# A decoder step on one core: a weight ring of four units instead of five, and sample attention over eight sequences in one go

## The chip, the core and the metric

The kernel runs on one core of a Trainium2 chip. The metric is device time of one execution in microseconds (us). A few per cent of the matmul records may be missing from a trace.

## The reference: what is computed

Two decoder layers work on 1024 new prompt tokens and on 8 sampled sequences of 8 tokens, all in float32 with a model width of 1024. In each layer x is normalized, mixed over tokens (layer 0: a gated linear recurrence, "rg"; layer 1: chunked gated linear attention, "gla"), then goes through cross-attention to 256 memory tokens in 4 heads of width 256, then through an MLP with a hidden width of 4096.

```python
def cross_attn(xn, k, v, w_q, w_o):
    q = (xn @ w_q).reshape(B, T, XA_HEADS, XA_HD)
    s = jnp.einsum('bthd,bmhd->bhtm', q, k) * (XA_HD ** -0.5)
    p = jax.nn.softmax(s, axis=-1)
    o = jnp.einsum('bhtm,bmhd->bthd', p, v).reshape(B, T, D_MODEL)
    return o @ w_o
...
x = x + mixer(rmsnorm(x, norm_mix_g[layer]))
x = x + cross_attn(rmsnorm(x, norm_xa_g[layer]), mem_k[layer], mem_v[layer], xa_wq[layer], xa_wo[layer])
hid = rmsnorm(x, norm_mlp_g[layer]) @ mlp_w1[layer]
x = x + jnp.square(jax.nn.relu(hid)) @ mlp_w2[layer]
```

The prompt attends to memory keys and values that this step computes from mem_prompt. Each of the 8 sampled sequences attends to its own cached keys and values (cache_mem_k, cache_mem_v), 256 KB a sequence and head for the keys and as much for the values.

## The kernel before, in words

All 1088 token columns stay resident as x transposed, in three chunks (c = 0, 1, 2) of 384, 384 and 320 columns; the last has 256 columns of the prompt and the 64 sampled ones. Each float32 GEMM is three matmuls, since operands are split into a high and a low part: high by high (L99), low by high (L100) and, with the low part of the weights, high by low (L101). Tiles xh and xl (or hh and hl) are the halves of the activations, whi and wlo those of the weights.

Weights come as units of 128 by 1024 floats (512 KB). `pump` loads a unit from HBM into a staging buffer `raw` (SP issues the DMA) and, as soon as the unit RING before it has been freed, splits it: ACT casts it to whi (L186), DVE subtracts to get wlo (L187). RING is the number of split units that fit (L145). There is one staging buffer of the ring's own, and each phase may add some of its own pool (`new_phase(name, more_raw)`). `get` hands out the next two units, `free` gives two back.

`gemm_in` (48 matmuls a chunk into the PSUM banks pa) makes a projection of a chunk. `gemm_out` (48 matmuls into pb) is the way back; DVE adds each of its groups into x (L279). Out projections aren't run where their operands are made: `queue_out` puts them on a list, and `pop` runs the oldest where the program wants work for PE. The phases run in the order memory keys and values, rg, attention 0, MLP 0, gla, attention 1, MLP 1. Instructions are issued in program order as far as the scheduling of the tile framework keeps it, and each engine runs its own in order.

The recurrence `rg` goes over four groups g of 256 channels. Per group and chunk there are X (a projection and a convolution), G (gates: 12 matmuls against gate weights gwh and gwl into the banks pm, then sigmoid, exp, tanh and square root on ACT, and a scan on DVE) and Y (a second projection, gelu, a product into hh and hl), and then an out projection is queued. ACT loads a table whenever the function's family changes. PE's clock can be granted at 2.4 GHz or at half of it; the profile gives it as a share of full speed.

The attention `xattn` goes over 4 heads h and 3 chunks c. Per item there are Q (projection), `scores` and softmax, `p_trans` (L774), `p_v`, and the queued out projection. The sampled columns are treated with the last chunk: `sample_s` multiplies each sequence's queries qs (padded to 32 columns) with its keys, `sample_p` is the softmax, `sample_v` transposes P (`turn`, L809), multiplies it as pt with the values and turns the result again. The product is `dot4` (L801): for four sequences side by side in the array's column quarters, two matmuls of 128 by 32 weights and 256 columns each; a matmul shows as two records. A key or value tile is `kvt`, loaded by `load` (L706); there are six such buffers, and the memory's own keys and values (out_mem_kT, out_mem_v) pass through them too.

```python
L798        def dot4(out, o, lhs, rhs):
L799            for s in range(2):
L800                for i in range(4):
L801                    nc.tensor.matmul(out[i * 32:i * 32 + 32, o * 256:o * 256 + 256], lhs(s, i), rhs[i][:, s, :],
L802                                     start=s == 0, stop=s == 1)
```

Of the kernel before, what the change touches and what calls it, by code (L numbers as in the profile page):

```python
# [8 lines left out]
F32 = mybir.dt.float32  # L9
# [13 lines left out]
NC = len(COL)  # L23
# [4 lines left out]
MAXW = max(WID)  # L28
# [19 lines left out]
class Step:  # L48
# [95 lines left out]

    RING = 5  # L145

# [378 lines left out]
    def rg(self, next_norm):  # L525
        nc, a = self.nc, self.a
        self.new_phase("rg")
        halo = self.t("halo", [128, 2, 3])
# [3 lines left out]
        def Y(us, us_o, g, c):  # L532
            p = self.gemm_in(us, c)
            if c == NC - 1:
                self.free(us)
            w = WID[c]
            z = self.t("gy", [128, 2, MAXW])[:, :, :w]
            for f in range(2):
                nc.vector.tensor_mul(z[:, f], p[f][:, :w], self.rstd[c])
            gelu = nc.scalar.activation(z, z, AF.Gelu_apprx_tanh)  # L540
            if (g, c) == (3, NC - 1):
                self.table(gelu)
            nc.vector.tensor_mul(z, z, xc.pop(c)[:, :, :w])
            hT = self.hidden()
            nc.scalar.copy(hT[0][:, :, :w], z)
            nc.vector.tensor_sub(hT[1][:, :, :w], z, f32(hT[0][:, :, :w]))
            self.queue_out(us_o, hT, c, next_norm if g == 3 else None)
# [81 lines left out]

        for g in range(4):  # L630
            us_x = self.get()
            us_o = []
# [7 lines left out]
            G(gw, g, 0)  # L640
            self.pop()
            us_y = self.get()
# [47 lines left out]
    def xattn(self, l, next_norm):  # L690
        nc, a = self.nc, self.a
# [5 lines left out]
        st = {}  # L697
# [4 lines left out]

        def load(src):

            t = self.t("kvt", [128, 2, 256], F32, 6)
            nc.sync.dma_start(t, src.rearrange("(t p) c -> p t c", p=128))  # L706
            return t

        def load_split(src, tag):
            raw = load(src)  # L710
            hi = self.t(tag + "h", [128, 2, 256], R32)
            lo = self.t(tag + "l", [128, 2, 256], R32)
            split(hi, lo, raw)
            return hi, lo
# [76 lines left out]

        def keys4(h, o):
            return [load(a.cache_kT[l, o * 4 + i, h]) for i in range(4)]

        def vals4(h, o):
            return [load(a.cache_v[l, o * 4 + i, h]) for i in range(4)]

        def dot4(out, o, lhs, rhs):  # L798
            for s in range(2):  # L799
                for i in range(4):  # L800
                    nc.tensor.matmul(out[i * 32:i * 32 + 32, o * 256:o * 256 + 256], lhs(s, i), rhs[i][:, s, :],  # L801
                                     start=s == 0, stop=s == 1)  # L802

# [8 lines left out]

        def sample_s(h, o, k4):
            if o == 0:
                st["s"] = self.pb()
            dot4(st["s"], o, lambda s, i: qs[:, s, o * 4 + i, :], k4)

# [4 lines left out]

        def sample_v(h, P, hT):
            p = turn(P)
            pt = self.t("pt", [128, 2, 2, 128])
            nc.scalar.copy(pt, p)
            so = self.pb()
            for o in range(2):
                dot4(so, o, lambda s, i: pt[:, s, o, i * 32:i * 32 + 32], vals4(h, o))
            ot = self.t("q", [128, 2, MAXW])[:, :, 0:256]  # L830
# [13 lines left out]
        for n, (h, c) in enumerate(items):  # L844
# [4 lines left out]
            tail = c == NC - 1  # L849
            if tail:  # L850
                k4 = keys4(h, 0)
            if nxt:
# [4 lines left out]
            if tail:  # L857
                sample_s(h, 0, k4)
                k4 = keys4(h, 1)
                sample_s(h, 1, k4)  # L860
                P = sample_p(h)
            else:
                self.pop()
# [5 lines left out]
            if tail:  # L869
                sample_v(h, P, hT)  # L870
                self.pop()
# [362 lines left out]
```

## Time and profile before

| what | before |
|---|---|
| median of 3 runs | 3126.18 us (3124.58 to 3127.01) |
| the profiled execution's own time | 3127.53 us |
| its span in the trace | 3125.8 us |
| mean granted clock of PE | 0.995 of full speed |
| loads and stores in HBM | 178.34 MB read, 13.52 MB written |
| memory keys and values | from 7.6 to 115 us |
| rg | to about 440 us |
| attention 0, MLP 0 | to about 715 us, to about 1480 us |
| gla, attention 1 | to about 2050 us, to about 2345 us |
| MLP 1 | to the end |

The stages' limits are read from PE's blocks in the timeline. PE, PEld, DVE, ACT, POOL and SP are the engines: matmuls, weight loads (they run beside matmuls), vector, scalar, the general engine and the one that issues DMAs. In the rows below, a timeline's row gives the start, the duration, the engine, the line, the operation, out<-in by tile names, sizes and a count of consecutive records; a pipelined matmul's duration is longer than the distance to the next one's start, so distances between starts are what adds up.

### The profile page before, as it was taken

Reading aid. Unit: us, or ns where it says so; the run is one execution under the profiler, and the core shown is the slowest. Engines: PE = TensorE matmul, PEld = TensorE weight load, DVE = VectorE, ACT = ScalarE, POOL = GpSimd, SP = SyncE. Lnnn points to the kernel's source line nnn. Section 1 sums busy time; section 2 is a strip of 40 time slices with the busy share of each in tenths; the row PEclk is TensorE's granted clock in tenths of the full one; section 3 lists DMA queues with packets and bytes.
Section 4 is the critical chain, followed back from the end, with each engine's and each line's share of the span. In section 5 each row is a group of like instructions: output and inputs, shape, how many; then the busy total and the mean of one; then the engine's idle time right before and its main releaser. Section 6 shows DMA issues by size and latency. Waiting matters only on the chain.

```text
span 3125.8 us, 46516 instructions
## 1 busy us (share of the span) xinstructions
PE 3072.0 (98%) x19319; PEld 2932.3 (94%) x19319; DVE 1743.6 (56%) x3266; ACT 1017.9 (33%) x1847; POOL 197.1 (6%) x274
## 2 busy tenths in 40 slices
PE   8999999999999999999999999999999999999997
PEld 7999989989999999999889888798989999999997
DVE  7577785566444444445454454675565444444445
ACT  7555572234211211113333233442243111111114
POOL 3111020001000000001000000010010000000002
PEclk9999999999999999999999999999999999999998
DMA  8311113331111111111011102023331111111111
GB/s 272 116 43 43 41 56 102 95 101 62 49 47 41 47 49 41 41 52 45 28 57 42 56 28 70 24 81 103 108 94 48 48 41 41 54 42 41 43 46 58
DMA packets 155779, 194.85 MB, mean 62 GB/s; under 512 B 11280, under 2 KB 140560, under 8 KB 155568
## 3 DMA queue, kind: packets, MB, share of 16 engines
q1 hardware_dynamic: 152768, 182.82, 18.8%
q0 software_dynamic: 2800, 9.06, 0.8%
q8 instruction: 151, 2.47, 0.3%
q14 instruction: 60, 0.49, 0.1%
HBM read 178.34 MB, written 13.52 MB: 61 GB/s over the span
## 4 chain that ended last, share of the span: by engine, by line
PE 88%; DVE 4%; DMA 3%; ACT 3%; issue 1%; POOL 0%; SPq 0%; DVEq 0%; ACTq 0%; POOLq 0%
PE pa L100 11%; PE pa L99 11%; PE pa L101 11%; PE pb L99 9%; PE pb L101 8%; PE pb L100 8%; PE pm L99 4%; PE pm L100 4%; PE pm L101 4%; PE pa L262 2%; PE pa L264 2%; PE pa L263 2%; PE pb L801 1%; PE pm L1034 1%; DVE wlo L187 1%
## 5 line engine op out<-in xcount | busy, mean ns | idle before, releaser
L100 PE MATMUL pa<-xl,whi 128*128 128x384 f32 (+2 forms) x2336 | 762.4, 326 | 4.4 <-DVE xl L312 4.4
L99 PE MATMUL pa<-xh,whi 128*128 128x384 f32 (+2 forms) x2336 | 762.2, 326 | 2.9 <-DVE xs L565 1.5
L101 PE MATMUL pa<-xh,wlo 128*128 128x384 f32 (+2 forms) x2336 | 761.2, 326 | 0.0
L279 DVE TENSOR_TENSOR x<-x,pb 128x384 f32<-128x384 f32 (+1 forms) x792 | 411.2, 528 | 228.8 <-PE pb L101 228.4
L99 PE MATMUL pb<-hh,whi 128*128 128x384 f32 (+1 forms) x1584 | 523.5, 332 | 2.4 <-DVE x L279 2.4
L100 PE MATMUL pb<-hl,whi 128*128 128x384 f32 (+1 forms) x1584 | 520.7, 329 | 0.0
L101 PE MATMUL pb<-hh,wlo 128*128 128x384 f32 (+1 forms) x1584 | 518.3, 328 | 0.0
L186 ACT CAST whi<-raw 128x1024 fp32r<-128x1024 f32 (+1 forms) x250 | 257.4, 1041 | 666.0 <-PE pa L100 349.6
L187 DVE TENSOR_TENSOR wlo<-raw,whi 128x1024 fp32r<-128x1024 f32 (+1 forms) x250 | 304.4, 1228 | 264.1 <-ACT whi L186 263.2
L100 PEld LDWEIGHTS pa<-xl,whi 128*128 128x128 f32 x2336 | 439.0, 188 | 9.8 <-DVE xl L312 6.3
L99 PEld LDWEIGHTS pa<-xh,whi 128*128 128x128 f32 x2336 | 439.2, 188 | 8.5 <-issue 4.4
L101 PEld LDWEIGHTS pa<-xh,wlo 128*128 128x128 f32 x2336 | 439.2, 188 | 0.8 <-issue 0.8
L679 DVE SCALAR_TENSOR_TENSOR r<-pa,rstd 128x384 f32<-128x384 f32 (+1 forms) x192 | 102.2, 534 | 394.4 <-PE pa L101 394.3
L99 PEld LDWEIGHTS pb<-hh,whi 128*128 128x128 f32 x1584 | 297.6, 188 | 15.8 <-DVE x L279 7.8
L100 PEld LDWEIGHTS pb<-hl,whi 128*128 128x128 f32 x1584 | 298.4, 188 | 5.2 <-issue 4.9
L101 PEld LDWEIGHTS pb<-hh,wlo 128*128 128x128 f32 x1584 | 298.2, 188 | 3.8 <-issue 3.7
L680 ACT ACTIVATE r<-r 128x768 f32<-128x768 f32 (+1 forms) x96 | 77.6, 808 | 670.9 <-DVE r L679 670.9
L279 DVE TENSOR_TENSOR x<-x,pm 128x320 f32<-128x320 f32 (+1 forms) x360 | 190.9, 530 | 112.1 <-PE pm L101 111.8
L306 POOL TENSOR_TENSOR acc<-acc,sq 128x384 f32<-128x384 f32 (+1 forms) x105 | 115.7, 1102 | 2082.0 <-ACT sq L305 2051.6
L99 PE MATMUL pm<-hh,whi 128*128 128x320 f32 (+1 forms) x720 | 234.6, 326 | 0.0
L101 PE MATMUL pm<-hh,wlo 128*128 128x320 f32 (+1 forms) x720 | 234.5, 326 | 0.0
L100 PE MATMUL pm<-hl,whi 128*128 128x320 f32 (+1 forms) x720 | 234.5, 326 | 0.0
(305 smaller groups left out, 4356.9 us busy)
## 6 DMA issues: line engine op xcount, KB each, us to landing
raw<-in_mlp_w SPq DMA_DIRECT2D x128, 512.0 KB, 3.8
kvt<-in_cache_kT SPq DMA_DIRECT2D x64, 256.0 KB, 3.8
kvt<-in_cache_v SPq DMA_DIRECT2D x64, 256.0 KB, 3.7
raw<-in_xa_wv SPq DMA_DIRECT2D x16, 512.0 KB, 5.2
raw<-in_rg_w_in SPq DMA_DIRECT2D x16, 512.0 KB, 3.6
raw<-in_xa_wq SPq DMA_DIRECT2D x16, 512.0 KB, 3.5
raw<-in_xa_wo SPq DMA_DIRECT2D x16, 512.0 KB, 3.5
raw<-in_gla_w_in SPq DMA_DIRECT2D x16, 512.0 KB, 3.7
```

The lines of the kernel that those rows point to most:

```text
L99: mm(out, lh, rh, start=first, stop=False)
L100: mm(out, lh, rl, start=False, stop=False)
L101: mm(out, ll, rh, start=False, stop=last)
L186: nc.scalar.copy(hi[:, o], raw[:, o])
L187: nc.vector.tensor_sub(lo[:, o], raw[:, o], f32(hi[:, o]))
L262: mm(out, self.xh[c][:, k, xs], hv[:, kk, :], start=k == 0, stop=False)
L263: mm(out, self.xh[c][:, k, xs], lv[:, kk, :], start=False, stop=False)
L264: mm(out, self.xl[c][:, k, xs], hv[:, kk, :], start=False, stop=k == 7)
L279: nc.vector.tensor_add(x, x, p[:, :per * w].rearrange("p (m t) -> p m t", m=per))
L306: (nc.vector if m % 4 == 3 else nc.gpsimd).tensor_add(self.acc[c][:, :w], self.acc[c][:, :w], sq[:, :w])
L679: nc.vector.scalar_tensor_tensor(r[:, f], p[f][:, :w], 0.0, self.rstd[c], op0=OP.max, op1=OP.mult)
L680: nc.scalar.activation(r, r, AF.Square)
```

## The change

The ring of split weights has four units instead of five, which frees 8 KB in each of the 128 partitions. The attention has eight key and value buffers `kvt` instead of six; the memory's own keys and values pass through a buffer of their own, `kvr`. The sampled products of all eight sequences stand in one loop (`dots`, matmul at L800 now), for which all eight keys are loaded one chunk earlier and all eight values right behind the scores. In the recurrence the phase has a second staging buffer, `gy` has two buffers, and one of the three places where a queued out projection is run moves to the front of each group. Line numbers from 801 on become smaller by one to four.

```diff
--- before.py
+++ after.py
@@ -142,7 +142,7 @@
                 rows(a.mlp_w2[l], g * 256)
         self.units = u
 
-    RING = 5
+    RING = 4
 
     def pump(self, loads=None, also=None):
         nc = self.nc
@@ -524,7 +524,7 @@
 
     def rg(self, next_norm):
         nc, a = self.nc, self.a
-        self.new_phase("rg")
+        self.new_phase("rg", 1)
         halo = self.t("halo", [128, 2, 3])
         self.stage = self.t("stage", [128, NK, 36])
         xc, xcs = {}, {}
@@ -534,7 +534,7 @@
             if c == NC - 1:
                 self.free(us)
             w = WID[c]
-            z = self.t("gy", [128, 2, MAXW])[:, :, :w]
+            z = self.t("gy", [128, 2, MAXW], F32, 2)[:, :, :w]
             for f in range(2):
                 nc.vector.tensor_mul(z[:, f], p[f][:, :w], self.rstd[c])
             gelu = nc.scalar.activation(z, z, AF.Gelu_apprx_tanh)
@@ -628,6 +628,7 @@
                 nc.gpsimd.tensor_copy(st[:, :, 27:35], h[:, :, 256:320].rearrange("p f (b t) -> p f b t", b=8)[:, :, :, 7])
 
         for g in range(4):
+            self.pop()
             us_x = self.get()
             us_o = []
             X(us_x, g, 0)
@@ -638,7 +639,6 @@
             self.tick()
             self.pop()
             G(gw, g, 0)
-            self.pop()
             us_y = self.get()
             Y(us_y, us_o, g, 0)
             self.tick()
@@ -700,14 +700,14 @@
             nc.scalar.copy(ch, src)
             nc.vector.tensor_sub(cl, src, f32(ch))
 
-        def load(src):
-
-            t = self.t("kvt", [128, 2, 256], F32, 6)
+        def load(src, tag="kvt", bufs=8):
+
+            t = self.t(tag, [128, 2, 256], F32, bufs)
             nc.sync.dma_start(t, src.rearrange("(t p) c -> p t c", p=128))
             return t
 
         def load_split(src, tag):
-            raw = load(src)
+            raw = load(src, "kvr", 1)
             hi = self.t(tag + "h", [128, 2, 256], R32)
             lo = self.t(tag + "l", [128, 2, 256], R32)
             split(hi, lo, raw)
@@ -789,17 +789,16 @@
             return hT
 
 
-        def keys4(h, o):
-            return [load(a.cache_kT[l, o * 4 + i, h]) for i in range(4)]
-
-        def vals4(h, o):
-            return [load(a.cache_v[l, o * 4 + i, h]) for i in range(4)]
-
-        def dot4(out, o, lhs, rhs):
-            for s in range(2):
-                for i in range(4):
-                    nc.tensor.matmul(out[i * 32:i * 32 + 32, o * 256:o * 256 + 256], lhs(s, i), rhs[i][:, s, :],
-                                     start=s == 0, stop=s == 1)
+        def eight(cache, h):
+            return [load(cache[l, b, h]) for b in range(8)]
+
+        def dots(out, lhs, rhs):
+
+            for o in range(2):
+                for s in range(2):
+                    for i in range(4):
+                        nc.tensor.matmul(out[i * 32:i * 32 + 32, o * 256:o * 256 + 256], lhs(o, s, i),
+                                         rhs[o * 4 + i][:, s, :], start=s == 0, stop=s == 1)
 
         def turn(src):
 
@@ -810,23 +809,21 @@
                                         self.ident)
             return p.rearrange("p (s o c) -> p s o c", s=2, o=2)
 
-        def sample_s(h, o, k4):
-            if o == 0:
-                st["s"] = self.pb()
-            dot4(st["s"], o, lambda s, i: qs[:, s, o * 4 + i, :], k4)
+        def sample_s(h, keys):
+            st["s"] = self.pb()
+            dots(st["s"], lambda o, s, i: qs[:, s, o * 4 + i, :], keys)
 
         def sample_p(h):
             P = self.t("P", [128, 3, 256])[:, 0:2, :]
             softmax(st.pop("s"), P)
             return P
 
-        def sample_v(h, P, hT):
+        def sample_v(h, P, vals, hT):
             p = turn(P)
             pt = self.t("pt", [128, 2, 2, 128])
             nc.scalar.copy(pt, p)
             so = self.pb()
-            for o in range(2):
-                dot4(so, o, lambda s, i: pt[:, s, o, i * 32:i * 32 + 32], vals4(h, o))
+            dots(so, lambda o, s, i: pt[:, s, o, i * 32:i * 32 + 32], vals)
             ot = self.t("q", [128, 2, MAXW])[:, :, 0:256]
             nc.vector.tensor_copy(ot, so.rearrange("p (a b) -> p a b", a=2))
             p = turn(ot)
@@ -847,17 +844,16 @@
                 uo = None
             nxt = items[n + 1] if n + 1 < len(items) else None
             tail = c == NC - 1
-            if tail:
-                k4 = keys4(h, 0)
+            if c == NC - 2:
+                keys = eight(a.cache_kT, h)
             if nxt:
                 self.need(nxt[1], norm)
                 Q(*nxt)
                 self.tick()
             p_trans(h, c)
             if tail:
-                sample_s(h, 0, k4)
-                k4 = keys4(h, 1)
-                sample_s(h, 1, k4)
+                sample_s(h, keys)
+                vals = eight(a.cache_v, h)
                 P = sample_p(h)
             else:
                 self.pop()
@@ -867,7 +863,7 @@
                     st["k"] = load_split(a.mem_kT[l, nxt[0]], "k")
                 scores(*nxt)
             if tail:
-                sample_v(h, P, hT)
+                sample_v(h, P, vals, hT)
                 self.pop()
             if uo is None:
                 uo = self.get()
```

How instructions move, at three places. First PE in the attention, the end of the scores of head 1 in layer 0 (kvt are keys, qs padded queries, hh and vh the prompt's P and memory values, xh and whi those of the next query projection). Before:

```order
L99 MATMUL pa<-xh_90,whi 128x384
L801 MATMUL pb<-kvt,qs 32x256
L100 MATMUL pa<-xl_93,whi 128x384
L101 MATMUL pa<-xh_90,wlo 128x384
L99 MATMUL pa<-xh_90,whi 128x384
L100 MATMUL pa<-xl_93,whi 128x384
L101 MATMUL pa<-xh_90,wlo 128x384
L801 MATMUL pb<-kvt,qs 32x256 x5
L99 MATMUL pa<-xh_90,whi 128x384
```

In the changed kernel, from the end of the query projection on:

```order
L101 MATMUL pa<-xh_89,wlo 128x384
L774 MATMUL pm<-ident,P 128x128 x4
L800 MATMUL pb<-kvt,qs 32x256 x16
L99 MATMUL pm<-hh,vh 128x256
L100 MATMUL pm<-hl,vh 128x256
L101 MATMUL pm<-hh,vl 128x256
L99 MATMUL pm<-hh,vh 128x256
```

The sixteen matmuls that stood as ten, one and five between GEMM matmuls stand in one row. Behind it there are 12 `p_v` matmuls, 12 score matmuls, 2 of the query projection, 6 of the scores, the transposes of P, 12 of the query projection, and then the sixteen for the values. Before, 29 matmuls of the query projection stood between the first scores piece and the first values piece, and now 14.

Second, SP's queue in the attention, one head (raw are weight units). Before:

```order
L706 DMA kvt<-in_cache_kT 128x2x256 x2
L706 DMA kvt<-out_mem_kT 128x2x256
L706 DMA kvt<-in_cache_v 128x2x256 x8
L706 DMA kvt<-out_mem_v 128x2x256
L706 DMA kvt<-in_cache_kT 128x2x256 x6
L165 DMA raw<-in_mlp_w 128x4x256 x2
```

In the changed kernel:

```order
L706 DMA kvr<-out_mem_v 128x2x256
L706 DMA kvt<-in_cache_v 128x2x256 x8
L706 DMA kvr<-out_mem_kT 128x2x256
L706 DMA kvt<-in_cache_kT 128x2x256 x8
L173 DMA raw<-in_xa_wo 128x1024
L165 DMA raw<-in_xa_wq 128x4x256 x2
```

The eight keys go out in one row behind the values of the head before, and the eight values in one row behind the memory's values; each value load waits for the matmul of the scores that used its buffer.

Third, ACT in the recurrence, group 0 around the gates of chunk 1 (L600 are the sigmoids, L186 the casts of weight units, L545 the cast of Y's result). Before:

```order
L611 ACT_TABLE_LOAD
L611 ACTIVATE rt<-rt 128x768
L348 COPY rstd_97<-pm 128x320
L186 CAST whi<-raw 128x1024
L600 ACT_TABLE_LOAD
L600 ACTIVATE rt<-pm,vec 128x384
L600 ACTIVATE it<-pm,vec 128x384
L600 ACTIVATE rt<-pm,vec 128x384
L600 ACTIVATE it<-pm,vec 128x384
L545 CAST hh<-gy 128x768
```

In the changed kernel:

```order
L611 ACT_TABLE_LOAD
L611 ACTIVATE rt<-rt 128x768
L348 COPY rstd_97<-pm 128x320
L186 CAST whi<-raw 128x1024 x2
L600 ACT_TABLE_LOAD
L600 ACTIVATE rt<-pm,vec 128x384
L600 ACTIVATE it<-pm,vec 128x384
L545 CAST hh<-gy 128x768
L600 ACTIVATE rt<-pm,vec 128x384
L600 ACTIVATE it<-pm,vec 128x384
```

Two casts of weight units, where one stood, are now ahead of the sigmoid's table load, and Y's cast stands between the sigmoids.

## Rows read from the trace of the kernel before

**Rows 1.** The page: busy time and share of the span by engine.

```profile
PE 3072.0 (98%) x19319; PEld 2932.3 (94%) x19319; DVE 1743.6 (56%) x3266; ACT 1017.9 (33%) x1847; POOL 197.1 (6%) x274
```

**Rows 2.** Waits of PE, whole span: us in total, times, longest us.

```profile
PE pb L801 <- DMA kvt<-in_cache_v: 1.3, 2, 0.9
...
PE pb L801 <- DMA kvt<-in_cache_kT: 0.5, 3, 0.2
```

**Rows 3.** Timeline of PE, layer 0, values of head 1: start us, duration us, instruction.

```profile
581.28 0.33 PE L99 MATMUL pa<-xh,whi 128*128 128x384 f32 x1
581.45 0.34 PE L100 MATMUL pa<-xl,whi 128*128 128x384 f32 x1
581.74 1.49 PE L801 MATMUL pb<-kvt,pt 128*32 128x256 f32 x20
...
583.44 0.34 PE L100 MATMUL pb<-hl,whi 128*128 128x384 f32 x1
...
585.37 0.34 PE L99 MATMUL pb<-hh,whi 128*128 128x384 f32 x1
585.64 0.62 PE L801 MATMUL pb<-kvt,pt 128*32 128x256 f32 x2
...
586.47 0.34 PE L101 MATMUL pb<-hh,wlo 128*128 128x384 f32 x1
...
586.84 0.34 PE L100 MATMUL pb<-hl,whi 128*128 128x384 f32 x1
587.11 1.05 PE L801 MATMUL pb<-kvt,pt 128*32 128x256 f32 x10
...
588.36 0.34 PE L99 MATMUL pb<-hh,whi 128*128 128x384 f32 x1
```

**Rows 4.** Timeline of PE, scores of the same head.

```profile
568.99 1.49 PE L801 MATMUL pb<-kvt,qs 128*32 128x256 f32 x20
...
572.82 0.62 PE L801 MATMUL pb<-kvt,qs 128*32 128x256 f32 x2
...
574.46 1.05 PE L801 MATMUL pb<-kvt,qs 128*32 128x256 f32 x10
```

**Rows 5.** Timeline of SP's queue, value loads of the same head.

```profile
571.57 12.14 SPq L706 DMA_DIRECT2D kvt<-in_cache_v  x8
```

**Rows 6.** Windows: length, busy us (PE, PEld, DVE, ACT, POOL), PEclk, DMA share, GB/s.

```profile
40.00:60.00 20.00, 14.46 (x105) 14.29 (x104) 16.48 (x25) 15.11 (x30) 9.10 (x9) 0.84 0.98 329
499.70:505.30 5.60, 5.42 (x40) 3.48 (x34) 1.72 (x3) 1.07 (x4) 0.00 (x0) 1.00 0.61 187
505.30:511.20 5.90, 5.90 (x42) 5.90 (x42) 3.60 (x10) 3.08 (x12) 0.00 (x0) 1.00 0.69 222
506.00:511.00 5.00, 5.00 (x38) 5.00 (x37) 2.75 (x9) 2.48 (x11) 0.00 (x0) 1.00 0.80 256
```

**Rows 7.** A split and a GEMM's start in the MLP (timeline); a load (page).

```profile
904.13 1.23 DVE L187 TENSOR_TENSOR wlo<-raw,whi 128x1024 fp32r<-128x1024 f32 x1 [0.45 <-ACT whi L186]
...
911.34 0.33 PE L99 MATMUL pa<-xh,whi 128*128 128x384 f32 x1
...
raw<-in_xa_wq SPq DMA_DIRECT2D x16, 512.0 KB, 3.5
```

**Rows 8.** Recurrence: timelines of ACT and PE, one window (columns as in rows 6).

```profile
153.94 1.05 ACT L186 CAST whi<-raw 128x1024 fp32r<-128x1024 f32 x1
155.01 1.28 ACT L600 ACT_TABLE_LOAD   x1
...
272.73 0.44 PE L99 MATMUL pb<-hh,whi 128*128 128x384 f32 x1 [0.41 <-DVE x L279]
...
159.30:162.80 3.50, 3.50 (x13) 3.50 (x13) 3.50 (x11) 3.47 (x5) 1.72 (x3) 0.51 0.42 140
```

**Rows 9.** Start of the kernel: timelines of DVE and PE.

```profile
51.30 1.77 DVE L187 TENSOR_TENSOR wlo<-raw,whi 128x1024 fp32r<-128x1024 f32 x1
...
55.16 0.87 PE L347 MATMUL pm<-ident,rtok 128*128 128x128 f32 x3 [5.54 <-DVE rtok L330]
```

## What the change does to the time: a prediction

> **What bounds the kernel now.** I read the page's busy times first. TensorE (PE) is busy 98% of the span, every other engine 56% or less [rows 1]; the idle rest is 3125.8 − 3072.0 = 54 us. Read alone, that row says that no change can win more than 54 us. But a busy PE need not be a full PE, so the second view is what it waits for where the change works: the attention's sample dots at L801 wait 1.8 us in all for their DMAs [rows 2]. A change that only removed these waits would win 1.8 us.
>
> So third, the timeline of PE where the change works. A GEMM matmul of 384 columns starts 0.17 us after the one before it (581.28 to 581.45) [rows 3]. The sample dots use a quarter of the array each (128x32) and run side by side. Their records come as pieces of 20, 2 and 10 (two records to a matmul) with GEMM matmuls between [rows 3, 4]. A piece costs what the start-to-start distance of the GEMM matmuls around it exceeds the usual 0.173: for 20 records 583.44 − 581.45 − 0.35 = 1.64 us, for 2 records 586.47 − 585.37 − 0.35 = 0.75, for 10 records 588.36 − 586.84 − 0.35 = 1.17: 3.56 us for 16 matmuls [rows 3]. They fit a fixed 0.32 for a piece and 0.22 for each step of up to four matmuls side by side and two records deep (6, 2 and 4 steps: 1.64, 0.76, 1.20). PE shows as busy in all of it: the gain, if there is one, lies inside the busy time.
>
> The Trainium skill says so too, in Perfetto Trace Analysis, section Identifying the Most-Contended Engine: matmul busy share is no good measure of the distance to the limit, and weight-load busy share is one of the better ones. Here that share is 94%, which leaves 194 us [rows 1]; by the rule 54 us is no ceiling, by the busy row it is.
>
> **The change, part by part.** *Sample dots in one go.* Sixteen matmuls back to back are 8 steps instead of 12, and one piece instead of three: 1.64 + 2 × 0.22 = 2.08 us instead of 3.56, so 1.5 us a block. In the scores the pieces of 2 and 10 are cut in the same way [rows 4]. There are 16 blocks (2 layers, 4 heads, scores and values): −24 us. Bounds: had the one piece to be priced by the row of 20 records pro rata, it were 1.64 × 32 / 20 = 2.62 and the gain 0.94 a block, −15 us; if scores save 0.1 more a block, which I could not price as cleanly, −25. I take −24, since three sizes of piece lie on one line. The 1.8 us of waits for these DMAs go too, since all keys are now loaded one chunk ahead: −1.8.
>
> *Values behind the keys.* Keys and values now share eight buffers, so no value load may start before the scores' matmuls have released a key. Before, the value loads trickled in from SP for 12 us ahead of and around their use, in buffers that came free piecemeal [rows 5]. Now: let T0 be the start of the scores block. The first keys are free at T0 + 1.0 (four steps). When five loads went out together, 1.31 MB landed in 5.9 us from the first issue (222 GB/s), at 256 GB/s once running [rows 6], so eight take 5.9 + 3 × 0.262 / 0.256 = 9.0 us: the last lands at T0 + 10.0. When does PE want it? Before, the values started 581.74 − 568.99 = 12.75 us after the scores [rows 3, 4]; by the new order 15 GEMM matmuls (2.6 us) fewer stand between and the scores are 1.5 us shorter, so they start at T0 + 8.6, and the second four values are wanted four steps later, T0 + 9.5. Stall: 0.5 to 0.6 us a head, 8 heads: +5. Bounds: at the 329 GB/s of the start of the kernel the loads land by T0 + 1 + 0.8 + 6.4 = 8.2 and nothing is lost (0); at the 187 GB/s of 499.7 to 505.3 they take 11.2 us, a stall of 2.7 a head, +22 [rows 6]. I stay near 222, because that stretch holds the very same kind of load in bulk, and the 187 covers time in which SP waited for buffers.
>
> The Trainium skill states, in DMA: Bandwidth & Descriptors, a limit of about 358 GB/s for one core's share of the memory; by it eight loads would need an estimated 5.9 us, no stall would appear, and the sum would be 5 us lower. The trace here never held that rate over such a stretch, so I keep the measured one.
>
> *Softmax and turn.* Between the scores block and the transposes of P (L809) PE now has more work than before, not less, so they are not late.
>
> *Ring of four.* A unit's split (cast on ACT, 1.05 us [rows 8], subtraction on DVE, 1.23 us [rows 7]) now waits for the unit four before it instead of five. In the MLP the order on PE and DVE is unchanged, and each unit is split one unit later: the splits that ran to 904.13 + 1.23 = 905.36 become those of the block that starts at 911.34 [rows 7]; 6.0 us of cover, cost 0. In the attention 48 out, 12 value and 12 score matmuls (8.3 + 2.1 + 1.4 = 11.8 us) lie between the last use of one head's query weights and the first of the next head's; cast, subtraction, load of the second unit (3.5 us [rows 7]), cast and subtraction take 8.1: 3.7 us of cover, the tightest place I found. In the GLA the order moves no split behind its use. If the cover goes, PE waits at a GEMM block's first matmul for whi or wlo.
>
> *Recurrence.* One pop moves to the front of each group, the second raw slot loads earlier, gy has two buffers. The interleaved out blocks become whole ones, which costs PE nothing. The splits of the Y weights can now run only when the previous group's third out block has ended, and nine gate matmuls (1.6 us) are ahead of Y: a cast and a subtraction, 1.05 + 1.23, are hidden for 1.6 of 2.28 us, so +0.7 for groups 1 to 3, about +2. In group 0 two casts instead of one now stand ahead of the sigmoid's table load (1.28) on ACT [rows 8]: +1 for the cast, +1 or 2 for PE's slower clock after the longer wait (the granted clock was 0.51, half of full speed, in 159.3 to 162.8, after two waits there [rows 8]). Gone are the waits of 0.41 a group for x [rows 8], −0.8. Sum +4; bounds −1 (splits hidden, waits gone) and +10 (both Y units exposed in each group, 4 × 2.3 plus 1).
>
> *Start (memory keys and values).* In the new order the rtok chain on DVE stands ahead of a subtraction that took 1.77 us inside it, at 51.30; PE's wait for rtok there is 5.5 us [rows 9], and some 2 of it go: −2. Bounds −5 (3 us of a slower clock behind so long a wait, as in [rows 8], go as well) and +1 (PE wants rtok three matmuls earlier and finds nothing shorter).
>
> **Sum.** −24 − 1.8 + 5 + 4 − 2 = −18.8 us against the profiled execution's 3127.53, which lies 1.35 above the median of 3126.18: 3108.7 there, **3107 us** as a median.
>
> **Rivals.** (A) *The values come late.* The eight loads start together behind the scores, with no second set to load into; at 187 GB/s the stall is 2.7 us a head, +22 instead of +5: 3124 us, within 0.2%. For it: SP issues one every 0.4 us and loads share the DMAs with weights. Against: 219 to 256 GB/s wherever loads went out in bulk. The Trainium skill's page Trainium Kernel Development and Optimization, Best Practices, says to double-buffer so that loads overlap compute; keys and values in one set of eight give this up. Wholly exposed, 9 us a head, it would be +72 and 3174 us; the 8.6 us of PE work between the blocks exclude that here. Chance 0.10.
>
> (B) *The recurrence pays for the room: slower.* One mechanism: in each group, at Y's first matmul, both casts, both subtractions and two table loads on ACT are in series behind the third out block: 2.1 + 2.4 + 2.6 = 7.1 us, less 1.6 of cover, and 3.4 us of half clock behind it as at 159.3: 8.9 a group, 36 us. That gives 3126.2 − 22.8 + 36 = 3139. It decides from (22.8 + 6.3) / 4 = 7.3 us a group. Against: the second cast overlaps the first subtraction, and ACT is busy a third of the time. Chance 0.06.
>
> (C) *One go is not cheaper by step.* The pro rata price holds, −15 instead of −24: 3116. Chance 0.12. (D) *The loads are in time* at 329 GB/s: 3102. Chance 0.15. That the dots are not joined is excluded by the new order, which has sixteen in a row.
>
> **How the numbers follow.** Forecast 3107 at 0.57, D 0.15, C 0.12, A 0.10, B 0.06. A measurement of this kernel tells 0.2%, 6.3 us, from no change: faster is under 3119.9, slower over 3132.4. Forecast, C and D are faster, but for a tail where the recurrence's +10 comes with C: 0.82; A and that tail are same: 0.12; B: 0.06. Range: low end D with the recurrence at −1, 3097; high end the forecast with the values at 1.6 us a head (+8) and the recurrence at +10, or C with half of either, 3121. It leaves out B and most of A.
>
> **What would show it.** Right: L800 with 32 records in one row, 1.9 to 2.1 us start to next; a wait of PE at L800 for in_cache_v of 0.3 to 1.2 us in each head; PE busy down by over 20 us; MLP stages as long as before; a wait of under 1 us for wlo at Y. Wrong: the attention's two stages not shorter by 17 to 24 us together (dots or loads mis-priced), or waits for whi or wlo over 2 us in the recurrence or the MLP.

## The result and the profile after

The changed kernel takes 3104.26 us (median of 4 runs, 3102.21 to 3104.96) beside 3125.91 us (4 runs) for the kernel before: a ratio of 0.9927, 95% interval 0.9915 to 0.994, so 21.7 us or 0.7% faster. Beside the last four experiments it was timed again: 3103.56 us beside 3129.56, so 26.0 us and a ratio of 0.9917 [0.9904, 0.9931].

Both traces were cut into stages at the record that transposes the last 64 tokens' rtok (L347, 64 by 64), which stands once in each normalization of x; the first part of a stage's GEMMs thus lies in the stage before, and the 9.8 us behind the last cut are the same in all three. There is one profile of the kernel before. Times in us:

| stage | before | after | change again (e11) |
|---|---|---|---|
| start, memory keys and values | 145.46 | 142.11 | 142.15 |
| recurrence | 333.51 | 332.68 | 331.67 |
| attention 0 | 274.49 | 266.50 | 266.07 |
| MLP 0 | 757.90 | 757.90 | 757.88 |
| gla | 576.77 | 577.03 | 576.46 |
| attention 1 | 277.42 | 267.28 | 269.76 |
| MLP 1 | 750.45 | 749.64 | 749.80 |

The attention's two stages give 18.1 us (16.1 in the second profile), the start 3.4, the recurrence 0.8 (1.8). MLP 0, where the ring of four was expected to cost nothing, is the same to 0.02 us, and MLP 1 is 0.6 to 0.8 us shorter. The span is 3102.9 us, the profiled execution 3104.66. The page of the changed kernel, busy time by engine:

```profile
PE 3050.6 (98%) x19319; PEld 2930.7 (94%) x19319; DVE 1743.2 (56%) x3266; ACT 1016.2 (33%) x1847; POOL 193.6 (6%) x274
```

PE is busy 21.4 us less than in [rows 1], and idle 52.3 us instead of 53.8. Nearly all that was gained was shown as busy before.

The waits of PE over the whole span (total, times, longest):

```profile
PE pm L347 <- DVE rtok L330: 7.3, 3, 4.4
...
PE pm L99 <- ACT rt L600: 3.0, 1, 3.0
PE pm L774 <- DVE P L747: 2.8, 2, 1.4
...
PE pb L99 <- ACT hh L545: 1.0, 1, 1.0
```

There is no row for L800 and a DMA among PE's waits any more (in [rows 2] there were two, 1.8 us). The rtok wait lost 3.6 us. New is a wait of 1.4 us in each layer for the prompt's P (L774 <- L747).

PE's timeline in the attention, head 0 and head 3 of layer 0 (heads are counted from 0):

```profile
494.54 1.93 PE L800 MATMUL pb<-kvt,qs 128*32 128x256 f32 x32
496.40 0.39 PE L99 MATMUL pm<-hh,vh 128*128 128x256 f32 x1
...
497.93 0.28 PE L761 MATMUL pm<-kh,qh 128*128 128x256 f32 x1
...
503.16 3.14 PE L800 MATMUL pb<-kvt,pt 128*32 128x256 f32 x32
506.23 0.44 PE L99 MATMUL pb<-hh,whi 128*128 128x384 f32 x1
...
695.73 0.70 PE L774 MATMUL pm<-ident,P 128*128 128x128 f32 x4 [1.40 <-DVE P L747]
...
699.94 0.34 PE L99 MATMUL pa<-xh,whi 128*128 128x384 f32 x1
700.21 1.93 PE L800 MATMUL pb<-kvt,pt 128*32 128x256 f32 x32
...
702.36 0.33 PE L100 MATMUL pb<-hl,whi 128*128 128x384 f32 x1
```

The scores are one row of 32 records, 1.86 us from start to the next start, where [rows 4] had three pieces. The values of head 3 show the price of a joined block by the recipe of [rows 3]: 702.36 − 699.94 − 0.35 = 2.07 us, forecast 2.08. But the values of head 0 take 506.23 − 503.16 = 3.07 us for the same 32 records, with no wait printed. The view of weight loads (PEld) of the same stretch says why:

```profile
503.16 1.01 PEld L800 LDWEIGHTS pb<-kvt,pt 128*32 128x32 f32 x20 [0.28 <-ACT pt L824]
504.52 0.14 PEld L800 LDWEIGHTS pb<-kvt,pt 128*32 128x32 f32 x2 [0.35 <-DMA kvt<-in_cache_v]
505.25 0.57 PEld L800 LDWEIGHTS pb<-kvt,pt 128*32 128x32 f32 x10 [0.60 <-DMA kvt<-in_cache_v]
```

The records of the second four sequences wait 0.35 and 0.60 us for value loads. Four steps of 0.22 us after the block's start, at 504.04, they were wanted, and the last wait ends at 505.25: 1.2 us later, which is the whole of the extra length. PE's records of this time are folded into one busy row. Over the eight heads the values blocks last 3.07, 3.10, 3.26, 1.86, 2.96, 2.29, 2.58 and 1.86 us: 6.1 us more than eight times 1.86. All of it is in the first three heads of each layer; in the last head PE comes to the values 11.7 us after the scores began instead of 8.6 to 8.7, and there is no wait. SP's queue and the data rate (slices of 0.3 us from 494 us on) in head 0:

```profile
495.62 3.95 SPq L706 DMA_DIRECT2D kvt<-in_cache_v  x8
501.19 0.37 SPq L706 DMA_DIRECT2D kvr<-out_mem_kT  x1
504.24 4.88 SPq L706 DMA_DIRECT2D kvt<-in_cache_kT  x8
```

```profile
GB/s 0 0 0 0 0 0 0 0 20 123 99 335 341 379 365 266 287 229 249 246 273 314 355 358 359 365 359 358 341 352 372 352 348 270 85 20 24 79 167 167
```

```profile
496.00:504.20 8.20, 8.20 (x78) 6.99 (x68) 5.58 (x15) 4.03 (x14) 0.00 (x0) 1.00 0.90 282
```

The first value is issued at 495.62, 1.08 us after the scores began, and the last wait ends at 505.25, 10.7 us after they began: 9.6 us for eight loads, where 222 GB/s had given 9.0 and [rows 6] bounded 7.2 to 11.2.

### The profile page after: what moved, and what is told of

Its sections match the earlier page's. It is cut to its first block, busy times and chain, and to the rows that moved or that the text cites. A ratio compares the mean times of both kernels' runs of the same rounds, so it can differ in the third digit from the quotient of the medians.

```text
span 3102.9 us, 46542 instructions
## 1 busy us (share of the span) xinstructions
PE 3050.6 (98%) x19319; PEld 2930.7 (94%) x19319; DVE 1743.2 (56%) x3266; ACT 1016.2 (33%) x1847; POOL 193.6 (6%) x274
## 4 chain that ended last, share of the span: by engine, by line
PE 91%; DVE 4%; ACT 2%; DMA 2%; issue 1%; POOL 0%; SPq 0%; DVEq 0%; ACTq 0%; POOLq 0%
PE pa L101 12%; PE pa L99 12%; PE pa L100 12%; PE pb L99 9%; PE pb L100 9%; PE pb L101 9%; PE pm L99 5%; PE pm L100 5%; PE pm L101 4%; PE pa L262 2%; PE pa L264 2%; PE pa L263 2%; DVE xl L312 1%; DMA kvt<-in_cache_v 1%; PE pm L1030 1%
## 5 line engine op out<-in xcount | busy, mean ns | idle before, releaser
L101 PE MATMUL pa<-xh,wlo 128*128 128x384 f32 (+2 forms) x2336 | 761.9, 326 | 0.0
L101 PE MATMUL pb<-hh,wlo 128*128 128x384 f32 (+1 forms) x1584 | 517.7, 327 | 0.0
L186 ACT CAST whi<-raw 128x1024 fp32r<-128x1024 f32 (+1 forms) x250 | 256.7, 1040 | 693.0 <-PE pa L100 349.2
L101 PEld LDWEIGHTS pa<-xh,wlo 128*128 128x128 f32 x2336 | 439.4, 188 | 0.6 <-DVE wlo L187 0.6
L99 PEld LDWEIGHTS pb<-hh,whi 128*128 128x128 f32 x1584 | 297.5, 188 | 16.8 <-DVE x L279 7.2
L101 PEld LDWEIGHTS pb<-hh,wlo 128*128 128x128 f32 x1584 | 298.0, 188 | 0.5 <-issue 0.4
L101 PE MATMUL pm<-hh,wlo 128*128 128x320 f32 (+1 forms) x720 | 234.5, 326 | 0.0
```

What stands on the lines that cost most here:

```text
L99: mm(out, lh, rh, start=first, stop=False)
L101: mm(out, ll, rh, start=False, stop=last)
L186: nc.scalar.copy(hi[:, o], raw[:, o])
```

## The experiments

Each kernel is timed against the kernel before on its own chip; that stood at 3128.6 us for e1 to e4, 3129.0 for e5 to e8 and 3129.6 for e9 to e12.

| run | median us | ratio to before [95%] | start | recurrence | attention 0 + 1 |
|---|---|---|---|---|---|
| e1 | 3116.36 | 0.9959 [0.9947, 0.9972] | 142.5 | 340.7 | 534.4 |
| e2 | 3120.43 | 0.9977 [0.9966, 0.9988] | 143.8 | 331.7 | 551.6 |
| e3 | 3131.17 | 1.0011 [1.0002, 1.0019] | 141.0 | 342.0 | 551.7 |
| e4 | 3121.11 | 0.9975 [0.9966, 0.9984] | 140.3 | 331.3 | 550.9 |
| e5 | 3099.11 | 0.9903 [0.9889, 0.9916] | 141.3 | 331.8 | 529.3 |
| e6 | 3100.61 | 0.9907 [0.9894, 0.9921] | 141.2 | 331.3 | 529.9 |
| e7 | 3102.69 | 0.9916 [0.9902, 0.9929] | 141.2 | 331.7 | 534.4 |
| e8 | 3111.28 | 0.9940 [0.9927, 0.9954] | 141.6 | 331.7 | 539.7 |
| e9 | 3109.14 | 0.9934 [0.9922, 0.9947] | 141.4 | 335.9 | 535.4 |
| e10 | 3105.49 | 0.9925 [0.9911, 0.9938] | 141.9 | 332.7 | 535.6 |
| e11 | 3103.56 | 0.9917 [0.9904, 0.9931] | 142.2 | 331.7 | 535.8 |
| e12 | 3103.64 | 0.9919 [0.9906, 0.9933] | 141.5 | 331.7 | 535.1 |

My theory with the trace in hand: the joined products earn some 24 us in busy time, the shared buffers give 6 back, and the recurrence is worth little either way. The rival: the ring and the new order of the recurrence make or cost a good part of it.

### The parts apart: e1, e2, e3

e1 is the change with the recurrence put back:

```diff
-        self.new_phase("rg", 1)
+        self.new_phase("rg")
...
-            z = self.t("gy", [128, 2, MAXW], F32, 2)[:, :, :w]
+            z = self.t("gy", [128, 2, MAXW])[:, :, :w]
...
-            self.pop()
             us_x = self.get()
...
             G(gw, g, 0)
+            self.pop()
```

> Ring of four and the attention part of the change; the recurrence as it was before (no second staging buffer, one gy, the pop in its old place). The trace of the change shows the recurrence 1 us shorter than before, so by the trace this kernel should take about 3105 to 3106 us. By the forecast's step (the recurrence part costs 4 us) it should take about 3100. Rival: the old recurrence needs the fifth unit, and with four it waits for whi or wlo at each group; then 3110 or more, with such waits of PE between 115 and 440 us.

e2 is the reverse, the kernel before with RING = 4 and these three edits:

> Ring of four and the recurrence part; the attention as it was before (six buffers, four sequences at a time). If the attention's joined products earn what the trace shows (18 us of the 22), this takes 3120 to 3123 us, with the start of the kernel some 3 us shorter. Rival: the gain came from the ring's and the recurrence's new order, and this kernel is at 3110 or below. Other rival: with four units the old attention loses, 3128 or more.

e3 is one line:

```diff
-    RING = 5
+    RING = 4
```

> The kernel before with four units instead of five and nothing else. If the 3 us at the start of the kernel come from the ring (a subtraction that leaves the normalization's chain on DVE), the wait of PE for rtok near 50 us is 2 to 3 us instead of 5.5 here too, and the time is about 3122 to 3124, unless the recurrence loses some. Rival: the ring of four costs in the recurrence or the MLP, 3130 or more, and the other parts pay it back.

By medians the ring of four alone costs 2.6 us (e3; its interval begins just above no change), the recurrence's edits on top of it give 10.7 (e2 against e3), the attention's edits on top of it 14.8 (e1 against e3). The stages say where. The ring of four shortens the start by 4.5 us and lengthens the old recurrence by 8.5 (342.0 against 333.5); the MLP and gla don't change by more than 1.4. With the recurrence's edits, the same stage is 331.7. So the first theory's "worth little either way" was wrong as a statement about the parts: the rival of e1 came true. The small net of the recurrence is a loss of 7 to 8.5 us and a gain of 8 to 10 that cancel. e1's rows in group 2 show the loss (SP, ACT, PE):

```profile
302.46 0.37 SPq L165 DMA_DIRECT2D raw<-in_rg_w_in  x1
...
307.27 1.04 ACT L186 CAST whi<-raw 128x1024 fp32r<-128x1024 f32 x1 [0.72 <-DMA raw<-in_rg_w_in]
...
308.37 0.44 PE L99 MATMUL pa<-xh,whi 128*128 128x384 f32 x1 [1.54 <-ACT whi L186]
...
309.63 0.44 PE L101 MATMUL pa<-xh,wlo 128*128 128x384 f32 x1 [0.30 <-DVE wlo L187]
```

The second Y unit is issued only at 302.46, when the one staging buffer is free, and cast at 307.27; PE stands 1.54 us for the cast and 0.30 us for the subtraction behind it; in groups 1 and 3 the wait for the cast is 0.7 us. With a fifth unit the first of the pair is split before, and the second waits in the staging buffer. In all, PE waits 5.4 us for whi and wlo between 118 and 445 us in e1 and in e3, and not at all in the kernel before. Some waits for activations became shorter in return (those for xl took 4.4 us before, 1.7 and 1.2 now). A second part of the loss is the clock, which is granted at half (0.5) for 6.8 us of this stage in e1 and for 10.2 us in e3, instead of 3.4 us before.

### Which of the recurrence's edits repairs it: e9, e10

```diff
-        self.new_phase("rg", 1)
+        self.new_phase("rg")
```

> The changed kernel without the recurrence's second staging buffer. With four units, a pair of Y units can be split only when the previous out units are free; with one staging buffer the second of the pair can be loaded only after the first has been cast, 4 to 5 us later (issue at 302.46, cast at 307.27 in the run with the old recurrence). If that buffer is what repairs the ring of four, the recurrence takes 338 to 342 us instead of 331 to 333, +6 to +9 us in the time. Rival: the place of the pop repairs it, and this kernel is within 2 us of the change.

```diff
-            self.pop()
             us_x = self.get()
...
             G(gw, g, 0)
+            self.pop()
```

> The changed kernel with the pop back behind the gates of chunk 0. The third out block then ends right in front of Y's first block, so a cast and a subtraction (2.3 us) stand between the release and Y's first matmuls, with the second staging buffer in place: 1 to 2 us a group, three groups, +3 to +6 us if the place of the pop matters by itself. Rival: with two staging buffers the place of the pop is worth nothing, within 1 us of the change.

Without the second staging buffer the recurrence takes 335.9 us, 3 to 4 more than in the change, and the median is 5.6 higher than e11: half of what e1 had lost, less than I expected. With the pop in its old place, the recurrence takes 332.7, within 1 us; the rival stands, and the 1.9 us in the medians are not in this stage. So with the buffer, the pop's place is worth nothing that these runs can tell; without it, the pop's new place and the two gy buffers together still halve the loss. Both runs have the two gy buffers, so neither shows what these are worth, nor what the staging buffer or the pop is worth without them.

### Are eight buffers needed: e4

```diff
-        def load(src, tag="kvt", bufs=8):
+        def load(src, tag="kvt", bufs=6):
```

> The changed kernel with six key and value buffers instead of eight; the products of eight sequences still in one loop. The last two keys and values of a block can only be loaded once the block has released its first buffers, and a load takes 2 to 3 us from its issue, so if the order on PE stays joined, each of the 16 blocks waits 2 to 3 us more: 3104 + 32 to 48 less the 6 us that the values wait now, 3130 to 3146. If the order is cut into pieces again, the time is near that of the attention before, 3120 to 3126. Rival: joining the products is all of the gain and the buffers are not needed, 3104.

The order was cut again. PE's timeline, scores of head 1:

```profile
560.97 1.49 PE L800 MATMUL pb<-kvt,qs 128*32 128x256 f32 x20
...
564.89 0.62 PE L800 MATMUL pb<-kvt,qs 128*32 128x256 f32 x2
...
566.52 1.05 PE L800 MATMUL pb<-kvt,qs 128*32 128x256 f32 x10
```

The three pieces of [rows 4] are back, with the same 20, 2 and 10 records, although the program has one loop, with other work of PE where the seventh and eighth load would be waited for. The attention's 550.9 us are those of the kernel before (551.9), so 17 us of the change hang on the two buffers, and the loop alone is worth nothing. Whether eight buffers would do as much with the old loop of four sequences wasn't tried.

### The price of a piece: e8

The scores' matmuls after the first four are put on a list and issued one group at a time between the mm3 of `p_v`; the softmax of the samples follows `p_v`:

```diff
+                    if apart and o + s:
+                        self.hook.append(lambda o=o, s=s: piece(o, s))
+                    else:
+                        piece(o, s)
...
                     self.mm3(p[:, :pw], vh[:, mt, ds], vl[:, mt, ds], ph_[:, mt, :pw], pl[:, mt, :pw], mt == 0, mt == 1)
+                    if self.hook:
+                        self.hook.pop(0)()
```

> The changed kernel with the scores' sixteen matmuls issued as pieces of 4, 1, 3, 4 and 4 among the twelve p_v matmuls (all keys are there, eight buffers). By the forecast's price (0.32 a piece, 0.22 a step of up to four matmuls and two records) scores are 4 pieces and 2 steps dearer: 1.7 us a block, 8 blocks, +14 us; the values' wait may take up to 1 us a head more or less with it. By the pro rata price (a record costs the same in any piece) nothing changes but the values' wait, −4 to +8.

```profile
492.92 0.64 PE L802 MATMUL pb<-kvt,qs 128*32 128x256 f32 x8
...
493.81 0.62 PE L802 MATMUL pb<-kvt,qs 128*32 128x256 f32 x2
...
494.79 0.63 PE L802 MATMUL pb<-kvt,qs 128*32 128x256 f32 x6
...
495.91 0.64 PE L802 MATMUL pb<-kvt,qs 128*32 128x256 f32 x8
...
497.03 0.64 PE L802 MATMUL pb<-kvt,qs 128*32 128x256 f32 x8
...
498.06 0.28 PE L762 MATMUL pm<-kh,qh 128*128 128x256 f32 x1
...
689.08 1.93 PE L802 MATMUL pb<-kvt,qs 128*32 128x256 f32 x32 [0.61 <-DVE x L280]
```

From the scores' start to the first matmul of the next scores (498.06) it is 5.14 us here and 497.93 − 494.54 = 3.39 in the change for the same work: 1.75 us a block for four more pieces and two more steps, forecast 1.7. The pro rata price (C) is excluded. All eight values blocks last 1.86 us here; in the six heads that waited, the values have 1.7 us more to land. In the last head of each layer the order came out whole all the same (32 records in one row at 689.08), so six blocks were cut, not eight. 6 × 1.75 − 6.1 = 4.4 us were to be seen in the attention; it is 5.9 against the change's first profile and 3.9 against its second.

### The wait for the values: e5, e6, e7

e5 leaves out the 64 value loads (its sampled outputs are made from keys):

```diff
-                vals = eight(a.cache_v, h)
+                vals = keys
```

> The changed kernel without the value loads of the sampled sequences: the keys are used as values, so 64 loads of 256 KB are left out. In the trace of the change six of the eight values blocks last 2.3 to 3.3 us from start to start of the next work instead of 1.86, 6.1 us in all. If that is the wait for values behind the keys, all eight last 1.86 here and the attention's two stages are some 6 us shorter than in the change (533.8 to about 527.7 us). Rival: the blocks are long for another reason (the array's mode, pt late), and they stay as long.

```profile
501.37 1.93 PE L800 MATMUL pb<-kvt,pt 128*32 128x256 f32 x32
503.23 0.44 PE L99 MATMUL pb<-hh,whi 128*128 128x384 f32 x1
```

All eight blocks last 1.86 us, so the length was the wait for the loads. The attention is 4.5 us shorter than in the change's first profile and 6.5 than in its second, about the 6.1 and 6.4 us that the blocks waited there: the wait is all that the loads cost, although 16.8 MB of transfers went with them.

e6 gives the attention a ninth buffer:

```diff
-        def load(src, tag="kvt", bufs=8):
+        def load(src, tag="kvt", bufs=9):
```

> Nine key and value buffers instead of eight (there is room for one more): one value goes out a head ahead, seven behind the scores, and the memory's next key goes out behind them. One load is 0.26 MB, 0.75 us at the 350 GB/s that the change's trace shows while its values load, so each waiting values block should lose 0.7 to 0.8 us of its wait, 4 to 5 of the 6 us. Rival: the last value's landing is not what the block waits for, and nothing changes.

SP's queue of head 0 and PE's values of heads 0 and 1:

```profile
493.19 3.45 SPq L706 DMA_DIRECT2D kvt<-in_cache_v  x7
496.75 0.40 SPq L706 DMA_DIRECT2D kvt<-in_cache_kT  x1
```

```profile
500.73 1.98 PE L800 MATMUL pb<-kvt,pt 128*32 128x256 f32 x32
...
567.06 1.86 PE L800 MATMUL pb<-kvt,pt 128*32 128x256 f32 x22
...
569.20 1.05 PE L800 MATMUL pb<-kvt,pt 128*32 128x256 f32 x10 [0.29 <-DMA kvt<-in_cache_v]
```

Seven values go out behind the scores, and the eighth load there is a key of the next head. Six of the eight blocks last 1.86 to 1.93 us now, two 2.54 and 3.13: of 6.1 us of wait 4.1 are gone, and the attention takes 529.9 us, 3.8 to 5.9 less than with eight. The median is 3100.6, the lowest of the kernels here that compute everything; its interval overlaps the change's, so this step is shown by the stage and the blocks, not by the medians.

e7 gives the memory's own keys and values a second buffer, so that their load goes out ahead:

```diff
-            raw = load(src, "kvr", 1)
+            raw = load(src, "kvr", 2)
```

> Two buffers for the memory's own keys and values instead of one, so that the memory's next key goes out ahead of the eight values instead of behind them, while they are under way. If its 0.26 MB share the DMA engines with the values, the values land some 0.5 to 0.75 us earlier and 3 to 4.5 of the 6 us go. Rival: loads are served in the order of their issue, the key behind the values costs them nothing, and the values blocks last as long as in the change.

SP's queue of head 0 in e7:

```profile
493.67 3.96 SPq L706 DMA_DIRECT2D kvt<-in_cache_v  x8
499.24 0.37 SPq L706 DMA_DIRECT2D kvr<-out_mem_v  x1
```

The waits sum to 5.2 us instead of 6.1 and the attention takes 534.4. But this run doesn't separate the two: the memory's key did go out ahead, and the memory's values of the next head took its place behind the values, 5.57 us after the first of them as before (501.19 − 495.62). The difference of 0.9 us tells nothing either: e1, whose attention is that of the change, waits 5.0 us. What bears on the question is head 2 of each layer in the change's own profile:

```profile
630.05 3.95 SPq L706 DMA_DIRECT2D kvt<-in_cache_v  x8
638.76 3.45 SPq L706 DMA_DIRECT2D kvt<-in_cache_kT  x6
```

There no memory load follows the values, and they wait 1.40 and 0.72 us (0.79 and 1.42 in the second profile), as long as in heads 0 and 1, which have one (0.43 to 1.24, and 0.70 to 1.29). So the load behind the values costs them nothing that these traces can tell; what counts, by e6, is how many loads stand between the release and the last value.

### The last head: e12

```diff
+            if nxt is None:
+                self.pop()
             p_trans(h, c)
```

> Nine key and value buffers as in the run before, and in the last head of each layer one queued out projection is run ahead of the transposes of P, which waited 1.4 us for the softmax there. If that wait is what the last head gives back, 2.8 us go: some 7 us under the change and 3 us under nine buffers alone. Rival: the out projection is missing later, where it covered the sampled softmax and the next normalization, and the time is the same or longer than with nine buffers alone.

Waits of PE around the end of attention 0 (445 to 760 us):

```profile
PE pm L100 <- DVE hl L701: 1.2, 3, 0.8
PE pb L99 <- DVE x L279: 0.7, 1, 0.7
PE pm L336 <- DVE acc L306: 0.7, 1, 0.7
```

The wait of 1.4 us for P is gone, and 0.7 to 1.2 us each for hl, x and acc stand in its place. With nine buffers and this edit the attention takes 535.1 us, no better than with eight, although the values wait only 1.7 us. Most of the 5 us over e6 are lost in the last heads, where by these waits the out projection that was moved ahead is missing later: the rival holds, the two changes don't add, and by the attention's stages e6 is the better kernel (the medians' intervals overlap).

## Why the prediction came true, and where its steps did not

**Forecast 3107, measured 3104.3; range and sign held.** As a gain, some 19 us were forecast and 21.7 and 26.0 measured. Step by step:

- *The gain lies inside the busy time.* Shown: PE's busy time fell by 21.4 us, its idle time by 1.5. By the rule of the Trainium skill in Perfetto Trace Analysis, section Identifying the Most-Contended Engine, 54 us of idle were no ceiling; the trace agrees as far as it goes, since the gain came from elsewhere.
- *Joined blocks, −24 us and −1.8 of waits.* The price of a block was right (2.07 for 2.08), and e8 confirms the fixed cost of a piece from the other side (1.75 for 1.72). Rival C is out.
- *Values behind the keys, +5.* 6.1 us in the first profile, 6.4 in the second, and e5 shows that it is the loads. The sum was right to about a quarter, in part by luck: the wait was to be 0.5 to 0.6 us in each of eight heads, and it is 0.43 to 1.40 in six and nothing in two. In head 0 the last load landed 0.7 us later than T0 + 10.0, and PE came at T0 + 8.6 as worked out. The sign that was named, a wait of PE at L800, isn't in PE's rows; it stands in those of PEld. A and D are both out. By the limit of about 358 GB/s that the Trainium skill gives in DMA: Bandwidth & Descriptors, section Specifications, there would have been no wait; single slices of the trace do reach 350 to 379 GB/s, but the window of 8.2 us holds 282, and the measurement decides.
- *Softmax and turn are not late.* For the transposes of the samples' P (L808 now) this held. But the transposes of the prompt's P (L774) were not looked at: in the last head no scores of a next head stand between, and joining the samples' scores took PE there 1.4 us before the softmax had P. 2.8 us were given back. Sum for the attention: −24 − 1.8 + 6.1 + 2.8 = −16.9, measured −18.1 and −16.1; the second lies just outside the 17 to 24 us that the prediction named as its sign.
- *Ring of four, 0 in the MLP.* Right, to 0.02 us in MLP 0; so is the attention, where no wait for whi or wlo appeared. But I priced the ring and the recurrence's edits as one, and so missed that the ring of four costs the old recurrence 8.5 us (e3; 7.2 in e1).
- *Recurrence, +4.* Measured −0.8 and −1.8: the step that failed. "A cast and a subtraction are hidden for 1.6 of 2.28 us, so +0.7" assumed that splitting begins when the out block ends (217.01). ACT, DVE and PE there:

```profile
216.62 2.00 ACT L186 CAST whi<-raw 128x1024 fp32r<-128x1024 f32 x2 [17.64 <-PE pb L100]
...
217.70 2.36 DVE L187 TENSOR_TENSOR wlo<-raw,whi 128x1024 fp32r<-128x1024 f32 x2
...
218.60 0.34 PE L99 MATMUL pa<-xh,whi 128*128 128x384 f32 x1
...
218.98 0.44 PE L101 MATMUL pa<-xh,wlo 128*128 128x384 f32 x1
```

ACT begins at 216.62, while the out block's last matmuls still run, 0.4 us before its end; and wlo is wanted by the third matmul of Y's block, not by the first. These two make up the 0.7: PE's first L101 is some 0.03 us late, and so it is in groups 2 and 3. With both units staged, nothing of the split is exposed. In group 0 the wait for the sigmoid did grow by 1.0 us and Y's hh wait by 1.0 (0.5 in the second profile), as expected in kind, and so did the time at half clock, 6.8 us instead of 3.4:

```profile
155.90:162.70 6.80, 6.36 (x19) 6.04 (x20) 6.80 (x22) 5.17 (x9) 1.31 (x4) 0.50 0.46 147
```

The waits for x went, as forecast; but a wait of 1.3 us for xs went too, and those for xl at the end fell from 4.4 to 2.7, which I had not counted.
- *Start, −2.* −3.4, and −1.7 to −5.1 in the profiles of the twelve runs, all of which have a ring of four and the same order there, against the one profile of the kernel before. So the sign is right, and the size not settled to better than 2 us. Little of it comes from where I put it. The subtraction of 1.77 us left the chain, but a subtraction of the activations took a stretched 1.63 us in it:

```profile
49.93 1.63 DVE L312 SCALAR_TENSOR_TENSOR xl<-x,vec,xh 128x384 fp32r<-128x384 f32 x1
51.49 0.95 DVE L328 TENSOR_TENSOR irms<-irms,rtok 128x3 f32<-128x3 f32 x1
...
53.65 0.87 PE L347 MATMUL pm<-ident,rtok 128*128 128x128 f32 x3 [2.41 <-DVE rtok L330]
```

The chain from L327 to L330 on DVE is 3.6 us long instead of 4.0; it starts 1.2 us earlier, with one subtraction less ahead of it, and PE has rtok 1.5 us earlier. Nor is PE's wait the measure: in the change's second profile it is 4.4 us instead of 2.4, and the stage is as long (142.15 for 142.11). Another 1.5 us is a wait of the recurrence's first projection that the cut puts into this stage; it stands in the kernel before and in no profile with a ring of four:

```profile
127.56 0.45 PE L99 MATMUL pa<-xh,whi 128*128 128x384 f32 x1 [1.52 <-DVE xs L565]
```

So the total came out near because two errors had opposite signs: the recurrence and the start took 6 to 7 us less than forecast, the attention 3 to 5 us more. Rival B (the recurrence pays) was wrong for this change, but its mechanism, waits for Y's casts and subtractions and half clock behind them, is a good part of what e1 and e3 measured. Their loss is 7.2 and 8.5 us, 2.4 to 2.8 a group over three groups instead of 8.9. B also priced 3.4 us at half clock as 3.4 us lost; half speed loses half of that, some 1.7.

## What to carry to other kernels

A busy engine can still hold time: price an interruption from the starts of the regular work on both sides of it, and count the pieces, not only the records. When buffers decide whether a block can be issued whole, the loop in the program is not what counts; look at the order that results, and at how many loads stand between the release of the buffers and the last one needed. And price a change of a shared resource against the old code and the new code apart: a loss and its repair may hide each other.

## What was not expected of the hardware

- A wait inside a run of quarter-array matmuls is not shown in PE's row, which gives 3.14 us as one busy row of 32 records; the same wait stands in the weight loads' row (0.35 and 0.60 us).
- A ninth load, issued 5.6 us after the first value and before the last had landed, doesn't visibly slow the eight: the heads without it wait as long (1.40 and 0.72 us) as those with it (0.43 to 1.24 us).
- The start of the kernel varied from 140.3 to 143.8 us among the profiles with a ring of four, and the wait for rtok in it from 2.4 to 5.3 us (the change's first profile and e2; 4.4 in the change's second), with the same instructions in the same order on PE, DVE and ACT up to there. That is more than several of the effects looked for, so that stages had to be compared, not spans.
